# The indexer's scores by pairs of heads: a 128-row matmul each, then a 64-row matmul each, and one PSUM bank moved

## The chip, the cores and the metric

The kernel runs on one core of one Trainium2 chip. The metric is the time of one execution on the device, in microseconds (us). A profile of one execution was taken by the hardware profiler; the engines are PE (TensorE, the matrix engine; PEld are its loads of the stationary operand), DVE (VectorE), ACT (ScalarE), POOL (GpSimd) and SP (SyncE, which here only issues transfers).

## The reference, cut to what matters

One layer of a transformer-like block over 2048 tokens: a first norm and a projection into conv, attention, indexer and pool branches, a sparse attention, an output projection, and a mixture of 32 experts. What is changed lies in the indexer, which picks for each query the 256 keys that attention then uses:

```python
def block(args):
    qa, qib, wib, bi = args
    qchunk = (bi * Q_BLOCK + jnp.arange(Q_BLOCK)) // CHUNK
    allowed = key_chunk[None, :] <= qchunk[:, None]
    rel = jax.nn.relu(jnp.einsum('bqhd,bsd->bqhs', qib, ki).astype(jnp.float32))
    score = jnp.einsum('bqhs,bqh->bqs', rel, wib.astype(jnp.float32)) * idx_scale
    score = jnp.where(allowed[None], score, -jnp.inf)
    _, idx = lax.top_k(score, topk)
...
```

There are 8 indexer heads of 64 channels, 16 tiles of 128 queries, and up to 2048 keys for the last tile.

## The kernel before, in words

The program has five stretches: the projections and the convolution (0 to about 407 us of the profile), the scores of the first tile that needs them ("ahead", inside the last part of the projections, until about 456), the attention (456 to 1225), the output projection and the router (to 1490), and the experts (to the end).

The attention goes over 16 tiles `t` of 128 queries in four groups `g` of two heads each. `attention()` weaves the steps of several generators: `logits(t, g)` of the next group (bank `pl`, three matmuls of `mm3`, lines 92 to 94, then line 1009 on DVE), `context(t, g)` of this group (transposes of line 1032 into bank `pt`, products of line 1044 into bank `pc`, and the 32-column products of line 1051), `scores` of the tile four places on, and `threshold` of tiles between. The tile framework then orders the instructions of each engine by a timeline that it models itself, so the order on PE isn't the order in which the code is written; `order` rows below show it.

`scores(t, S)` works on blocks of up to 512 keys. Queries and keys are held as a sum of two rounded parts, high and low. For an even head, `q[:, h, :]` has the high part on partitions 0 to 63 and the low part on 64 to 127; for an odd head the other way round (`sweep3`). `kk[0]` holds the high part of the keys on both halves of the partitions, `kk[1]` the low part on both. So the matmul of line 843 gives high·high + low·high, and that of line 844 adds high·low + low·low in the same bank. Then ACT takes the relu (line 846) and DVE adds it, weighted, to `S` (line 847).

PSUM has eight banks. The attention uses `pl` x3, `pi` x2, `pt` x2 and `pc` x1:

```python
ps = self.bank("pi", 2)
nc.tensor.matmul(ps[:, :e - s], q[:, h, :], self.kk[0][:, s:e], start=True, stop=False)
nc.tensor.matmul(ps[:, :e - s], q[:, h, :], self.kk[1][:, s:e], start=False, stop=True)
```

`repair()` holds a second copy of the scores' code, which runs only where a query's count of keys came out wrong; it isn't in the trace.

Of the kernel before, what the change touches and what calls it, by code (L numbers as in the profile page):

```python
# [42 lines left out]
def norm_inv(p):  # L43
    """quantile of the standard normal distribution"""
    return NormalDist().inv_cdf(p)


class K:
# [91 lines left out]
    def modulation(self, q, xp):  # L140
        """shift and scale of channels q*256.. by column of 128, for the first norm"""
        nc = self.nc
        acc = xp.tile([128, 2, 256], F32, name="macc", tag="macc", bufs=2)
        for j in range(4):
            w = xp.tile([128, 2, 2, 256], F32, name="modw", tag="xt", bufs=7)
            for m in range(2):
                o = m * D + q * 256
                self.last = nc.sync.dma_start(w[:, :, m], self.a["mod_w"][0, j * 256:(j + 1) * 256, o:o + 256]
                                  .rearrange("(k p) f -> p k f", p=128))
            for i in range(2):  # L150
                k = 2 * j + i
                if k == 0:
                    nc.vector.tensor_scalar(acc, w[:, i], self.cond[:, 0:1], None, op0=OP.mult)
                else:
                    nc.vector.scalar_tensor_tensor(acc, w[:, i], self.cond[:, k:k + 1], acc, op0=OP.mult, op1=OP.add)
        ps = self.cm()
        for m in range(2):
            for j in range(2):
                o = 2 * m + j
                nc.tensor.matmul(ps[:, o:o + 1], acc[:, m, j * 128:(j + 1) * 128], self.ones,  # L160
                                 start=(o == 0), stop=(o == 3), skip_group_check=True)
        s = slice(2 * q, 2 * q + 2)
        nc.vector.tensor_tensor(self.mod.rearrange("p (m k) -> p m k", m=2)[:, :, s],
                                ps[:, :4].rearrange("p (m k) -> p m k", m=2),
                                self.col("mod_b")[:, 0:16].rearrange("p (m k) -> p m k", m=2)[:, :, s], OP.add)
        nc.vector.scalar_tensor_tensor(self.A1[:, s], self.mod[:, 8 + 2 * q:10 + 2 * q], 1.0, self.col("norm1_g")[:, s],
                                       op0=OP.add, op1=OP.mult)

    def modrows(self, mp):
        """the other parts as rows: first gate, second shift and scale (with the norm's gain), second gate"""  # L170
        nc = self.nc
        for i in range(8):
# [13 lines left out]
            ps = self.bank("pl", 3)  # L186
# [18 lines left out]
    def front(self):  # L205
        """x -> normalised, transposed; w_in; conv and pool branches; keys, indexer and queries."""
# [27 lines left out]
    def load_w(self, cols):  # L234
        """column ranges of w_in side by side, [128, KT, n]"""
# [64 lines left out]
    def sweep1(self, c1, u, side):  # L300
        """conv and pool channels: u = a_val sigmoid(a_gate), and u_pool"""
# [88 lines left out]
    def query_weights(self, pool, st):  # L390
        """w_uq[c, h, :] . w_uk[k, h, :] / 8 with both norms' gains, split"""
# [35 lines left out]
    def sweep2(self, c1, side):  # L427
        """keys and values, the indexer's weights and keys, absorbed queries"""
# [14 lines left out]
        def load(t):  # L443
            """h of a tile of tokens"""
# [25 lines left out]
        def turn(c, m):  # L470
            """half of them with channels on partitions"""
# [60 lines left out]
    def spend(self, side, n, after=None):  # L532
        """steps of the convolution, where the engines are free"""
# [7 lines left out]
    def sweep3(self, c1, side):  # L541
        """the indexer's queries: per head, the split halves on partitions 0-63 and 64-127"""
# [32 lines left out]
    def conv(self, st, u):  # L575
        """causal depthwise convolution, layernorm over the channels, silu: a step per yield"""
# [80 lines left out]
    def poolmix(self, st, c, up):  # L657
        """causal moving averages of 2, 4, 8, 16 less the input, a 64x64 product per group"""
# [40 lines left out]
    def work(self, pool, width, dtype, tag, bufs):  # L699
        """a tile of the attention; for the tile of queries that is ahead of it, in the pool that is there"""  # L700
# [6 lines left out]
    def ahead(self):  # L707
        """selection of the first tile of queries that has more than 256 keys, by steps"""
# [36 lines left out]
    def attention(self):  # L745
        nc, tc = self.nc, self.tc
        with ExitStack() as c1:
# [9 lines left out]
            def scores(i):  # L757
                """of the tile at place i, 8 steps per 512 keys"""
# [7 lines left out]
            def bound(i):  # L766
                """its threshold, ten steps; the tiles without one have a plain mask"""
# [31 lines left out]
            for _ in rows:  # L799
# [4 lines left out]
                                   lambda: self.bank("pi", 2, (128, 2, 256)))  # L804
# [19 lines left out]
    def weave(self, *parts):  # L824
        """steps of several generators evenly mixed; the last step of each is its rest"""
# [7 lines left out]
    def scores(self, t, S):  # L833
# [5 lines left out]
        for h in range(NH):  # L839
            for s in range(0, n, 512):  # L840
                e = min(s + 512, n)
                ps = self.bank("pi", 2)
                nc.tensor.matmul(ps[:, :e - s], q[:, h, :], self.kk[0][:, s:e], start=True, stop=False)  # L843
                nc.tensor.matmul(ps[:, :e - s], q[:, h, :], self.kk[1][:, s:e], start=False, stop=True)  # L844
                r = self.work("ap", 512, F32, "rel", 3)
                nc.scalar.activation(r[:, :e - s], ps[:, :e - s], AF.Relu)  # L846
                nc.vector.scalar_tensor_tensor(S[:, s:e], r[:, :e - s], self.wi[:, t, h:h + 1],  # L847
                                               S[:, s:e] if h else self.tie[:, s:e], op0=OP.mult, op1=OP.add)
                yield
# [6 lines left out]
    def plain(self, t):  # L856
        """all the allowed keys, where they are no more than 256"""
# [5 lines left out]
    def threshold(self, t, S):  # L863
        """256 best: counts at moving thresholds until one has 248 to 263 scores above it, then the eight
        next below it or the eight least above it; queries for which that fails are marked"""
# [57 lines left out]
        # from the upper end down (sign 1), or from the lower end up (sign -1) where that is near enough  # L923
# [6 lines left out]
        # which of the eight: 256 - count down, count - 255 up  # L930
# [22 lines left out]
    def repair(self):  # L953
        """tiles with a query whose count is not 256: the selection in order of score and index, and again
        the attention"""
        nc, ap, tc = self.nc, self.ap, self.tc
        ps = self.bank("pl", 3)
# [30 lines left out]
    def logits(self, t, g):  # L988
        """masked logits of two heads, less their maximum, exponentials and their sums"""
# [12 lines left out]
        for h in (2 * g, 2 * g + 1):  # L1002
            L = P[h % 2]
            mx = st[:, 4 * h:4 * h + nb]
            for i, s in enumerate(range(0, n, 512)):
                e = min(s + 512, n)
                ps = self.bank("pl", 3)
# [10 lines left out]
    def context(self, t, g):  # L1018
        """the weighted keys and values of two heads, their outputs"""
# [7 lines left out]
        for k2 in range(0, t + 1, 2):  # L1027
            ks = range(k2, min(k2 + 2, t + 1))
            pt = self.bank("pi" if self.kvs and k2 % 4 else "pt", 2, (128, 2, 2, 128))
# [34 lines left out]
    def output(self):  # L1064
        """mix @ w_out, residual, second norm, router and the experts' lists of tokens"""
# [101 lines left out]
    def mixed(self, c, mix, os_, y, bank):  # L1167
        """conv, attention and pool outputs of 256 tokens, channels on partitions, split"""
# [17 lines left out]
    def blank_lists(self, st):  # L1186
        """the experts' lists full of entries for the spare rows, which are zero"""
# [50 lines left out]
    def first_max(self, st, src, n, N):  # L1238
        """one-hot of the first maximum over the last axis of src [128, N, n], and the maximum"""
# [13 lines left out]
    def route(self, c, lg, st):  # L1253
        """experts and gates of a group of tiles of tokens; their entries go to the experts' lists"""
# [67 lines left out]
    def order(self, st):  # L1322
        """experts by falling number of tokens; the one that is always the first to be computed comes last"""
# [9 lines left out]
        # key: count and, of equal counts, the first expert; by rows over the experts, and as a column  # L1333
# [30 lines left out]
    def parts(self, n):  # L1364
        """n tokens cut into blocks of up to 128, and units of 32 or 64 that share the columns of TensorE with
        other columns of the weights"""
# [10 lines left out]
    def moe_tiles(self):  # L1377
        """the second gate over all the partitions, also by the column groups of the units"""
# [14 lines left out]
    def moe(self):  # L1393
        """the experts in turn, those that TensorE takes longer for mixed with those that the loads take longer
        for; beside the products of the last three the results of all
        the tokens are written, and then again those of the tokens of the three"""
# [72 lines left out]
    def add(self, x):  # L1469
        """the sums into the tokens' rows"""  # L1470
# [3 lines left out]
    def again(self, x):  # L1474
        """the rows of an expert's tokens with the sums so far"""
# [7 lines left out]
    def final_part(self, x, zz, add=False):  # L1483
        """the last norm of an expert's tokens"""
# [22 lines left out]
    def final_rows(self):  # L1507
        """the last norm of all the tokens, by 256"""
# [29 lines left out]
    def gather(self, x, e, N, first):  # L1538
        """the rows of an expert's tokens"""
# [26 lines left out]
    def flip(self, x):  # L1566
        """those rows transposed; those of the blocks also split"""
# [25 lines left out]
    def slot(self, shape):  # L1593
        """the one of eight slots that has been idle for longest; the attention and w_out had them before. Extra
        ones are where the halves of the weights go later"""
# [8 lines left out]
    def done(self, *ws):  # L1604
        """slots whose last use has been written"""
# [4 lines left out]
    def load(self, srcs):  # L1610
        """256 K weights"""
# [22 lines left out]
    def half1(self, m, x):  # L1634
        """half of the inner dimension of the products with w1 and w3 for the blocks, tokens stationary"""
# [25 lines left out]
    def units1(self, x):  # L1661
        """the products with w1 and w3 for the units: a group of TensorE's columns for each part of the hidden
        columns"""
# [21 lines left out]
    def third(self, x, add=True):  # L1685
        """the products with w2, gates, and the sums into the tokens' rows"""
# [59 lines left out]
    def overflow(self):  # L1746
        """experts with more tokens than their part of the plan: 128 at a time"""
# [51 lines left out]
```

## Time and profile before

| what | value |
|---|---|
| time, median of 3 runs | 2300.21 us (2296.73 to 2302.23) |
| span of the profiled execution | 2302.6 us |
| PE busy | 2131.6 us, 93% of the span |
| DVE busy | 1653.4 us, 72% |
| ACT busy | 1233.9 us, 54% |
| POOL busy | 901.8 us, 39% |
| scores on PE: blocks of one head with up to 512 keys | 296 in the attention and 8 before it |

The profiled execution's time is its span; it is 2.4 us (0.1%) above the median of the three runs. The busy time of PE is the union of matmul records, whose ends are modelled: a record of a 512-column matmul is about 0.39 us long, while the next one starts 0.23 us after it. So what a matmul costs is read from start to start.

### The profile page before, as it was taken

How to read it: one execution, taken by the hardware profiler on the slowest of the kernel's cores; microseconds unless marked ns; L12 is line 12 of the kernel's file. 1: busy time of each engine (PE TensorE's matmuls, PEld its weight loads, DVE VectorE, ACT ScalarE, POOL GpSimd, SP SyncE). 2: the span in 40 equal slices, each digit the busy share in tenths (PEclk: the TensorE clock that was granted, in tenths of full speed). 3: DMA queues.
4: the chain of work that ended last, by engine and by line, in shares of the span. 5: the costliest groups of instructions: out<-in, count | busy, mean ns of one | idle time of the engine just before them, and what ended most of it. 6: DMA issues, size and time to landing. Idle time of an engine off the chain costs nothing. (4 is left out here: it accounts for less than half of the span.)

```text
span 2302.6 us, 37318 instructions
## 1 busy us (share of the span) xinstructions
PE 2131.6 (93%) x12943; PEld 1649.6 (72%) x12944; DVE 1653.4 (72%) x3217; ACT 1233.9 (54%) x2078; POOL 901.8 (39%) x1618
## 2 busy tenths in 40 slices
PE   5899999989999999999998999389999999999984
PEld 4777888766777787778897887366776776666763
DVE  5695899578888888887676555585786766766574
ACT  4832331277766667667563222265665665655562
POOL 4532233568745432232000122323565454645344
PEclk9999999999999999999999999689999999999997
DMA  8737869632122232112005644689999999999895
GB/s 282 263 129 229 245 243 325 224 98 65 33 69 83 70 93 83 56 51 62 23 6 206 244 138 138 229 278 309 352 336 293 304 340 346 326 319 323 299 322 169
DMA packets 263902, 460.55 MB, mean 200 GB/s; under 512 B 27985, under 2 KB 123650, under 8 KB 263700
## 3 DMA queue, kind: packets, MB, share of 16 engines
q1 hardware_dynamic: 234324, 363.40, 46.8%
q0 software_dynamic: 26912, 85.19, 12.4%
q10 hardware_dynamic: 2464, 9.44, 1.0%
q8 instruction: 105, 1.72, 0.3%
q14 instruction: 97, 0.79, 0.1%
HBM read 355.48 MB, written 101.43 MB: 198 GB/s over the span
## 5 line engine op out<-in xcount | busy, mean ns | idle before, releaser
L1631 DVE TENSOR_TENSOR wl<-wr,wh 128x1024 fp32r<-128x1024 f32 x314 | 393.0, 1288 | 171.3 <-ACT wh L1630 170.8
L1630 ACT ACTIVATE wh<-wr 128x1024 fp32r<-128x1024 f32 x372 | 373.6, 1053 | 249.2 <-PE acc L94 186.1
L93 PE MATMUL acc<-wl,xh 128*128 128x512 f32 (+3 forms) x544 | 218.7, 403 | 4.9 <-POOL wl L1631 4.7
L92 PE MATMUL acc<-wh,xh 128*128 128x512 f32 (+3 forms) x544 | 216.0, 407 | 5.3 <-ACT wh L1630 3.0
L94 PE MATMUL acc<-wh,xl 128*128 128x512 f32 (+3 forms) x544 | 215.2, 399 | 0.0
L1044 PE MATMUL pc<-pT,kv 128*128 128x256 f32 x840 | 205.1, 385 | 7.2 <-DVE ot L1056 5.6
L1009 DVE CUSTOM_DVE_ANT_0 L<-pl,bias 128x512 f32<-128x512 f32 (+3 forms) x312 | 181.9, 605 | 34.5 <-PE pt L1032 17.2
L846 ACT ACTIVATE rel<-pi 128x512 f32<-128x512 f32 (+3 forms) x296 | 154.5, 548 | 66.0 <-PE pi L844 29.0
L847 DVE SCALAR_TENSOR_TENSOR S<-rel,wi,S 128x512 f32<-128x512 f32 (+3 forms) x259 | 171.3, 679 | 24.1 <-ACT rel L846 23.6
L1044 PEld LDWEIGHTS pc<-pT,kv 128*128 128x128 f32 x840 | 156.3, 192 | 35.8 <-DVE ot L1056 9.4
L1631 POOL TENSOR_TENSOR wl<-wr,wh 128x1024 fp32r<-128x1024 f32 x58 | 145.8, 2562 | 86.0 <-ACT wh L1630 82.8
L1014 ACT ACTIVATE L<-L,ast 128x128 f32<-128x128 f32 (+15 forms) x128 | 154.4, 1207 | 41.6 <-DVE ast L1013 41.4
L598 DVE SCALAR_TENSOR_TENSOR ac<-u,kc,ac 128x512 f32<-128x512 f32 x240 | 174.1, 769 | 0.1
L1032 PE MATMUL pt<-identr,L 128*128 128x128 f32 x968 | 148.3, 275 | 5.2 <-ACT pT L1042 4.5
L1042 ACT ACTIVATE pT<-pt 128x512 f32<-128x512 f32 (+1 forms) x224 | 124.0, 572 | 33.3 <-PE pt L1032 24.3
L843 PE MATMUL pi<-kk,qi 128*128 128x512 f32 (+3 forms) x296 | 127.6, 432 | 14.4 <-ACT rel L846 13.7
L92 PE MATMUL pl<-kvT,qa 128*128 128x512 f32 (+3 forms) x320 | 130.4, 408 | 6.9 <-DVE ast L1009 5.8
L1032 PEld LDWEIGHTS pt<-identr,L 128*128 128x128 f32 x968 | 115.0, 140 | 29.3 <-ACT pT L1042 8.6
L1681 POOL DMA_INDIRECT x_d<-yo,ent x32 | 95.3, 2977 | 89.2 <-DVE yo L1724 66.3
L92 PEld LDWEIGHTS acc<-wh,xh 128*128 128x128 f32 (+3 forms) x544 | 97.5, 182 | 42.6 <-ACT wh L1630 8.7
L93 PEld LDWEIGHTS acc<-wl,xh 128*128 128x128 f32 (+3 forms) x544 | 99.3, 183 | 36.3 <-POOL wl L1631 5.6
L94 PEld LDWEIGHTS acc<-wh,xl 128*128 128x128 f32 (+3 forms) x544 | 99.1, 183 | 27.5
(531 smaller groups left out, 5328.5 us busy)
## 6 DMA issues: line engine op xcount, KB each, us to landing
wr<-in_exp_w_dram SPq DMA_DIRECT2D x256, 512.0 KB
wr<-in_exp_w_dram SPq DMA_DIRECT2D x64, 1024.0 KB
h<-h_d SPq DMA_DIRECT2D x64, 512.0 KB
h_d<-h POOLq DMA_DIRECT2D x32, 512.0 KB
qa_d<-qa POOLq DMA_DIRECT2D x32, 512.0 KB
qa<-qa_d SPq DMA_DIRECT2D x16, 1024.0 KB
modr<-in_mod_w_dram SPq DMA_DIRECT2D x64, 256.0 KB
xt<-in_x_dram SPq DMA_DIRECT2D x16, 512.0 KB
```

Of the source, the lines that this page charges most:

```text
L92: mm(out, lh, rh, start=start, stop=False)
L93: mm(out, lh, rl, start=False, stop=False)
L94: mm(out, ll, rh, start=False, stop=stop)
L598: nc.vector.scalar_tensor_tensor(acc[j], src, kc[:, j, i:i + 1], acc[j], op0=OP.mult, op1=OP.add)
L846: nc.scalar.activation(r[:, :e - s], ps[:, :e - s], AF.Relu)
L847: nc.vector.scalar_tensor_tensor(S[:, s:e], r[:, :e - s], self.wi[:, t, h:h + 1], S[:, s:e] if h else self.tie[:, s:e], op0=OP.mult, op1=O ...
L1009: nc.vector.tensor_tensor_reduce(L[:, s:e], ps[:, :e - s], bias[:, s:e], 1.0, -3e38, OP.add, OP.max, mx[:, i:i + 1])
L1014: nc.scalar.activation(L[:, :n], L[:, :n], AF.Exp, bias=neg, accum_out=st[:, 40 + h:41 + h])
L1032: nc.tensor.transpose(pt[:, kt - k2, j], P[j][:, kt * 128:(kt + 1) * 128], self.ident)
L1044: nc.tensor.matmul(pc, self.kv[:, kt, :], pT[:, kt - k2], start=(kt == 0), stop=(kt == t))
L1630: nc.scalar.activation(H[:, s], W[:, s], AF.Copy)
L1631: (nc.gpsimd if pool else nc.vector).tensor_tensor(L[:, s], W[:, s], H[:, s].bitcast(F32), OP.subtract)
```

## The change

Two heads are now taken together, with two banks `pi`. First come the two matmuls over all 128 rows, as before, then for each head a matmul over the 64 rows on which that head has its high part: rows 0 to 63 for the even head, 64 to 127 for the odd one. The 64-row matmul gives high·low; the product low·low is no longer computed. The number of matmuls and their columns stay as they were. `pi` has three banks in place of two, and `pl` two in place of three, everywhere that these are used. The other lines of the diff only take comments away.

```diff
-        for h in range(NH):
+        mm = nc.tensor.matmul
+        for h in range(0, NH, 2):
             for s in range(0, n, 512):
                 e = min(s + 512, n)
-                ps = self.bank("pi", 2)
-                nc.tensor.matmul(ps[:, :e - s], q[:, h, :], self.kk[0][:, s:e], start=True, stop=False)
-                nc.tensor.matmul(ps[:, :e - s], q[:, h, :], self.kk[1][:, s:e], start=False, stop=True)
-                r = self.work("ap", 512, F32, "rel", 3)
-                nc.scalar.activation(r[:, :e - s], ps[:, :e - s], AF.Relu)
-                nc.vector.scalar_tensor_tensor(S[:, s:e], r[:, :e - s], self.wi[:, t, h:h + 1],
-                                               S[:, s:e] if h else self.tie[:, s:e], op0=OP.mult, op1=OP.add)
-                yield
+                ps = [self.bank("pi", 3)[:, :e - s] for _ in range(2)]
+                for i in range(2):
+                    mm(ps[i], q[:, h + i, :], self.kk[0][:, s:e], start=True, stop=False)
+                for i in range(2):
+                    r = slice(64 * i, 64 * i + 64)
+                    mm(ps[i], q[r, h + i, :], self.kk[1][r, s:e], start=False, stop=True)
+                for i in range(2):
+                    r = self.work("ap", 512, F32, "rel", 3)
+                    nc.scalar.activation(r[:, :e - s], ps[i], AF.Relu)
+                    nc.vector.scalar_tensor_tensor(S[:, s:e], r[:, :e - s], self.wi[:, t, h + i:h + i + 1],
+                                                   S[:, s:e] if h + i else self.tie[:, s:e], op0=OP.mult, op1=OP.add)
+                    yield
...
-                ps = self.bank("pl", 3)
+                ps = self.bank("pl", 2)
...
-            pt = self.bank("pi" if self.kvs and k2 % 4 else "pt", 2, (128, 2, 2, 128))
+            pt = self.bank("pi" if self.kvs and k2 % 4 else "pt", 3 if self.kvs and k2 % 4 else 2, (128, 2, 2, 128))
```

The same moves of a bank (`pl` 2, `pi` 3) are made in `modrows`, `repair` and the call of `mixed`. In the changed file, line 845 is the 128-row matmul, line 848 the 64-row one, 1037 the transposes (1032 before), 1049 the products with `kv` (1044 before) and 1056 the 32-column products (1051 before).

The first place is the start of the attention on PE, its first four matmuls of scores; `pi_...` is the bank of a head's block, `kk0` and `kk1` are the high and low keys, `pl_...` the bank of the logits. Before:

```order
L843 MATMUL pi_4208<-kk0_1770,qi_4206 128x512
L844 MATMUL pi_4208<-kk1_1771,qi_4206 128x512
L843 MATMUL pi_4214<-kk0_1770,qi_4206 128x512
L844 MATMUL pi_4214<-kk1_1771,qi_4206 128x512
L92 MATMUL pl_4268<-kvT0_1772,qa_4263 128x128
```

And in the change, the same place:

```order
L845 MATMUL pi_4208<-kk0_1770,qi_4206 128x512
L845 MATMUL pi_4209<-kk0_1770,qi_4206 128x512
L848 MATMUL pi_4208<-kk1_1771,qi_4206 128x512
L848 MATMUL pi_4209<-kk1_1771,qi_4206 128x512
L845 MATMUL pi_4220<-kk0_1770,qi_4206 128x512
L848 MATMUL pi_4220<-kk1_1771,qi_4206 128x512
L92 MATMUL pl_4268<-kvT0_1772,qa_4263 128x128
```

Here the first pair stands as the code has it, with its two 64-row matmuls one behind the other; the next head's two already stand alone.

The second place is on PE in the middle of the attention of the change, between the logits (`pl`), the 32-column products (line 1056) and the transposes (`pt`):

```order
L94 MATMUL pl_7034<-kvT0_1772,qa_6540 128x384
L1056 MATMUL pc_4204<-wv_3275,cT_6785 32x64 x8
L845 MATMUL pi_6942<-kk0_1770,qi_6660 128x512
L848 MATMUL pi_6942<-kk1_1771,qi_6660 128x512
L845 MATMUL pi_6983<-kk0_1770,qi_6660 128x512
L848 MATMUL pi_6983<-kk1_1771,qi_6660 128x512
L1037 MATMUL pt_6950<-identr_130,L_6820 128x128
```

The 128-row and the 64-row matmul of each head stand together, and a 128-row one lies between the two 64-row ones of a pair. Of the 304 matmuls of line 848 in the part that runs, 5 stand directly in front of another of them; 179 stand in front of a matmul of lines 845, 92 or 93, 101 in front of one of lines 1037, 1049 or 618 (transposes and the products with `kv`), 16 in front of line 1056 and 3 in front of line 187 (one column).

## Rows read from the trace of the kernel before

**Rows 1.** Busy time by stage: us, busy by engine (instructions), clock, DMA share, GB/s.
```profile
456.00:1046.00 590.00, 554.33 (x3559) 442.98 (x3559) 489.43 (x1283) 413.83 (x819) 277.18 (x942) 0.99 0.24 71
1046.00:1225.00 179.00, 177.66 (x1322) 157.03 (x1320) 122.30 (x311) 109.85 (x162) 16.09 (x75) 1.00 0.10 32
```

**Rows 2.** Waits of PE from 456 to 1046: us in total, times, longest.
```profile
PE pi L843 <- ACT rel L846: 13.7, 18, 3.1
PE pl L92 <- DVE ast L1009: 5.8, 11, 1.3
PE pc L1044 <- DVE ot L1056: 5.6, 7, 1.9
PE pt L1032 <- ACT pT L1042: 4.5, 6, 1.2
...
PE pl L187 <- DVE ast L1009: 0.2, 1, 0.2
```

**Rows 3.** The scores' matmuls by shape, 456 to 1046: xcount, busy us, mean ns.
```profile
L844 PE MATMUL pi<-kk,qi 128*128 128x512 f32 x224 | 88.8, 396 | 0.0
...
L844 PE MATMUL pi<-kk,qi 128*128 128x384 f32 x24 | 8.1, 338 | 0.0
...
L844 PE MATMUL pi<-kk,qi 128*128 128x256 f32 x24 | 6.8, 282 | 0.0
L844 PE MATMUL pi<-kk,qi 128*128 128x128 f32 x24 | 6.6, 275 | 0.0
```

**Rows 4.** Timeline of PE: start us, us, what (rows*columns), matrix, xcount.
```profile
567.58 0.60 PE L1032 MATMUL pt<-identr,L 128*128 128x128 f32 x4
568.11 0.41 PE L1051 MATMUL pc<-wv,cT 128*32 128x64 f32 x10
568.45 0.50 PE L843 MATMUL pi<-kk,qi 128*128 128x512 f32 x1
568.78 0.40 PE L844 MATMUL pi<-kk,qi 128*128 128x512 f32 x1
569.11 0.31 PE L1051 MATMUL pc<-wv,cT 128*32 128x64 f32 x6
569.35 0.50 PE L92 MATMUL pl<-kvT,qa 128*128 128x512 f32 x1
569.69 0.40 PE L93 MATMUL pl<-kvT,qa 128*128 128x512 f32 x1
569.93 0.39 PE L94 MATMUL pl<-kvT,qa 128*128 128x512 f32 x1
```

**Rows 5.** Timeline of PE's loads in the same stretch.
```profile
569.11 0.15 PEld L1051 LDWEIGHTS pc<-wv,cT 128*32 128x32 f32 x6 [0.36 <-issue]
569.35 0.19 PEld L92 LDWEIGHTS pl<-kvT,qa 128*128 128x128 f32 x1
569.46 0.19 PEld L93 LDWEIGHTS pl<-kvT,qa 128*128 128x128 f32 x1
```

**Rows 6.** Timeline of PE: two transposes over 31 rows, then 128-row matmuls.
```profile
98.12 0.31 PE L583 MATMUL cm<-identr,kr 31*128 31x31 f32 x2
98.35 0.50 PE L92 MATMUL sm<-h,wh 128*128 128x512 f32 x1
98.69 0.40 PE L93 MATMUL sm<-h,wh 128*128 128x512 f32 x1
98.92 0.39 PE L94 MATMUL sm<-h,wl 128*128 128x512 f32 x1
```

**Rows 7.** Timeline of PE: 64-row products of line 419, then transposes.
```profile
235.41 2.79 PE L419 MATMUL sm<-ukT,uqT 64*128 64x128 f32 x32 [1.74 <-DVE ukT L410]
238.13 0.66 PE L483 MATMUL sm<-identr,z 128*128 128x128 f32 x4
```

**Rows 8.** Busy time of line 419 on PE: stretch, us, busy (matmuls), clock, DMA.
```profile
235.93:236.50 0.57, 0.57 (x12) 1.00 1.19 299
...
235.40:236.00 0.60, 0.59 (x6) 1.00 1.15 289
```

**Rows 9.** DVE's costliest lines that read the bank of the logits, 456 to 1046.
```profile
L1009 DVE CUSTOM_DVE_ANT_0 L<-pl,bias 128x512 f32<-128x512 f32 (+3 forms) x226 | 127.8, 585 | 7.7 <-PE pl L94 6.7 <-DMA y_d<-ac 0.6 <-PE pt L1032 0.2
...
L1009 DVE DVE_READ_ACCUMULATOR2_ANT ast<- 128x1 f32 x234 | 19.0, 81 | 0.0
```

More of the change, by code (lines that the diff above doesn't have):

```diff
@@ L803, in attention @@
                                    ap.tile([128, 4, 256], F32, name="cj", tag="cj", bufs=3),
-                                   lambda: self.bank("pi", 2, (128, 2, 256)))
+                                   lambda: self.bank("pi", 3, (128, 2, 256)))
             self.W = [self.w_cut(self.w_load(k, ap), self.ats, *tag) for k, tag in enumerate((("S", 3), ("R", 1)))]
@@ L956, in repair @@
         nc, ap, tc = self.nc, self.ap, self.tc
-        ps = self.bank("pl", 3)
+        ps = self.bank("pl", 2)
         nc.tensor.matmul(ps[0:1, 0:NT], self.ones, self.bad, start=True, stop=True)
@@ L1006, in logits @@
                 e = min(s + 512, n)
-                ps = self.bank("pl", 3)
+                ps = self.bank("pl", 2)
                 self.mm3(ps[:, :e - s], q[:, h, 0], q[:, h, 1], self.kvT[0][:, s:e], self.kvT[1][:, s:e], True, True)
```

## The prediction

> **What bounds the kernel now.** I read busy time by stage first. The scores run between 456 and 1046 us; in these 590 us PE is busy for 554, DVE for 489, ACT for 414 [rows 1]. Then comes what PE waited for: its waits, ten entries, sum to 34.7 us, which is nearly the whole of its 35.7 idle, and the longest entry is the scores' own bank, 13.7 us until ACT's relu had emptied it [rows 2]. So the stage is PE's, with some 6% of slack, and what PE spends longer is paid nearly in full. The weights of the experts come into buffers that the attention uses until its end, so a longer attention moves all that follows; I expect no change in the length of later stages.
>
> What one matmul costs is read from start to start. Within the logits, line 93 starts at 569.69 and line 94 at 569.93: 0.24 us for 512 columns, with the load of the stationary operand hidden beside the matmul before [rows 4]. In the scores there are 304 blocks, 296 in this stage (224 with 512 columns, three times 24 with 384, 256 and 128) [rows 3] and 8 with 384 columns before it.
>
> **The change part by part.** Matmuls, columns, relus and sums stay as many as they were. What could be saved is the overlap of the two 64-row matmuls of a pair. That such matmuls do overlap the trace shows in line 419, the only 64-row products: with one half of the rows at work 6 start in 0.60 us, with both halves 12 in 0.57 [rows 8]. If all 152 pairs did so, one half matmul of each would vanish: 112 pairs at 0.23 us, 16 at 0.175, 12 at 0.12 and 12 at 0.06, 30.7 us in all (0.23 scaled by columns). But a 128-row matmul needs both halves, and in the order of the change one lies between the two of a pair in all but 5 pairs. The saving is then 5 x 0.2 = 1 us.
>
> What it adds is a change of how the array is divided, from 128 rows to 64 and back, at each of the 299 places where 64-row matmuls begin and end. The trace of before has such changes at the 32-column products. Line 844 starts at 568.78, line 1051 behind it at 569.11: 0.33 in place of 0.23 to 0.24, so PE pauses 0.10 before the first 32-column matmul [rows 4]. On the way back line 92 starts at 569.35 and line 93 at 569.69, 0.34 in place of 0.24: the load of line 92 begins only at 569.35 and that of line 93 at 569.46, so 0.10 of load lies open which is hidden elsewhere [rows 4, 5]. The 31-row transposes do the same: the second starts near 98.20 and has at most 0.06 of work, line 92 starts at 98.35, and line 93 0.34 behind it, against 0.23 from there to line 94 [rows 6]. And at the end of the 64-row products: the last record ends at 238.20 and is 0.27 long, so it starts at 237.93; the transposes start 0.20 later, where 128 columns cost 0.11 [rows 7, 8]. That is the same pause of 0.09, though a wait on PE's own semaphore stands there too. That four transposes then take 0.66, against 0.60 in line 1032, prices the open load before them at 0.06 [rows 4, 7].
>
> One page speaks against the change outright: the Trainium skill, "TensorEngine Tiling (Array Packing)", section "Tiling Modes", says that a change of tiling mode, other than a change of tile, drains the engine. The pauses at 32 columns and 31 rows agree with it; it names no price, and the entry into 64 rows behind a 128-row matmul is in no row here. By the rule there is a pause at every entry and exit, without it none.
>
> I take the entry like that into 32 columns, since the exits of rows and columns agree to about 0.01 us: pause 0.10 and open load 0.10. The sum:
>
> - 299 entries x 0.20 = 59.8 us (no load can hide, since the 64-row operand can't be loaded while the array still works on 128 rows).
> - Exits: 179 in front of lines 845, 92, 93 x 0.20 = 35.8; 101 in front of transposes and the products with kv x (0.10 + 0.06) = 16.2; 19 in front of line 1056 or 187, which pause already, 0.
> - Overlap in 5 pairs: -1.
>
> Together +111 us. Bounds of one switch: below, nothing, if a change of rows costs nothing in one direction; above, the 0.20 that the rows show.
>
> What hides of it: a pause that falls where PE waits anyway is free. The waits are 35 us [rows 2], and as PE gets 18% more to do while ACT and DVE keep their work, waits shrink. Between 0 and 35 I take half, -18. The third bank `pi` aims at the 13.7 us of these and is in that bound.
>
> The second bank `pl` that is left: DVE takes 0.585 + 0.081 = 0.67 us per block on average [rows 9], PE's three matmuls about 0.70 for 512 columns; the wait for it is 5.8 us now [rows 2]. Nothing at the low end; at the high end the read of the accumulator, 0.08, lies open in each of 226 blocks, 18 us. In the new order matmuls of other lines, now slower, lie between, so I take +3. From 1046 to 1225, where logits run without scores, PE is busy for 177.7 of 179 [rows 1] with DVE at 122, so there is little to win and a few us to lose, within the same bound.
>
> Sum: 111 - 18 + 3 = +96. The profiled execution (2302.6) gives 2398.6; it stands 2.4 above the median of 2300.2, to which I set the forecast: **2396 us**.
>
> **The rivals.**
>
> *Faster: the halves overlap without a pause.* All 152 pairs give 30.7 us: 2270. Line 419 speaks for it, with a half that starts while the other works [rows 8]; it needs the two 64-row matmuls of a pair behind one another, and the order has that in 5. It decides if the array lets a 64-row matmul run beside a 128-row one on the other half. Of packing into rows, the Trainium skill, "TensorE: Matmul & The Clock Gate", "Part 3: Packing small matmuls", reports 3.07 times the speed with four row tiles. That holds for tiles one behind the other; by it all pairs overlapping would give this rival's time, and rows 8 agree with a factor near 2 for two halves.
>
> *Nothing: rows switch without a pause.* The 64-row matmul then costs what the 128-row one does, since the columns are the same, and only the banks and 1 us of overlap count: -14 from `pi` to +18 from `pl`, so 2286 to 2318, about 2299. For it: the entry into 64 rows isn't shown. Against it: the exit is, twice [rows 6, 7].
>
> *Half: only the exit, or only the entry, pauses.* 52 or 60 us, less the half of the waits: 2300 + 56 - 18 + 3 = 2341. For it, again, that only exits are seen with rows; against it, that with columns both directions pause [rows 4].
>
> *Slower through the banks alone* would be the upper end of the second rival, 2318.
>
> **How the numbers follow.** Pauses at both ends 0.80, one end 0.08, none 0.07, overlap 0.05. The first alone reaches from 2300 + 111 - 35 = 2376, a little lower if waits of the third bank vanish with it (2362), to 2300 + 111 + 18 = 2429. To leave out no more than 2 in 10 the range goes down to the half case: 2341 to 2429. The time of this kernel can be told from no change at about 0.2% (4.6 us); of the case without pauses I give 0.02 to faster, 0.03 to the same and 0.02 to slower. So faster 0.07, same 0.03, slower 0.90.
>
> **What would show it.** In the timeline of PE line 848 starts, with its load, about 0.33 after a line 845 that had its load hidden and 0.43 after one that came out of a switch itself (0.23 if nothing pauses); the matmul behind line 848 starts 0.43 after it, and its own successor 0.34 later. The stage of the scores grows from 590 to about 685 us, while the stages behind it keep their lengths; the waits of line 845 for ACT get fewer. The five pairs that stand together start their halves within about 0.01 us. The prediction is wrong if line 848 follows at 0.23 (no pause), or if PE's waits for `pl` come to more than 18 us; and if the clock, 0.99 of full in this stage [rows 1], falls in the pauses, the time is above the range.

## The result, and the profile after

The changed kernel takes 2364.5 us (median of 4 runs, 2358.2 to 2370.8) against 2300.4 us of before measured beside it: 1.0277 times, 95% interval 1.0254 to 1.0300, so 64 us slower. The forecast was 2396 in a range of 2341 to 2429, slower with a chance of 0.90. The direction and the mechanism came out; the size was 32 us too large. The times in this text leave out the slow executions, of which there were two, both of the logits' bank alone (2430 and 2651 us, at a granted clock of 0.84 and 0.75 where the others have 0.97). The two executions that the profiles show, of 2302.6 and 2359.5 us, lie 57 us apart: the one of before was a little longer than its median, the one of the change a little shorter.

The timeline of PE in the middle of the scores of the changed kernel (start us, us, what; line 848 is the 64-row matmul):

```profile
700.06 0.50 PE L845 MATMUL pi<-kk,qi 128*128 128x512 f32 x1
700.49 0.50 PE L848 MATMUL pi<-kk,qi 64*128 64x512 f32 x1
700.91 0.50 PE L92 MATMUL pl<-kvT,qa 128*128 128x512 f32 x1
701.25 0.39 PE L93 MATMUL pl<-kvT,qa 128*128 128x512 f32 x1
701.47 0.39 PE L94 MATMUL pl<-kvT,qa 128*128 128x512 f32 x1
...
704.13 0.39 PE L845 MATMUL pi<-kk,qi 128*128 128x512 f32 x1
704.45 0.50 PE L848 MATMUL pi<-kk,qi 64*128 64x512 f32 x1
704.88 2.43 PE L1049 MATMUL pc<-pT,kv 128*128 128x256 f32 x10
```

Read from start to start. Behind a line 845 that comes out of the logits, and so had its load hidden, line 848 starts after 0.32 (704.13 to 704.45), not after 0.23: the pause. Behind one that comes out of a switch itself it starts after 0.43 (700.06 to 700.49). The matmul behind line 848 starts 0.42 to 0.43 later, and line 93 starts 0.34 behind line 92, against 0.22 from there to line 94. PE's loads in the same stretch say why:

```profile
700.48 0.18 PEld L848 LDWEIGHTS pi<-kk,qi 64*128 64x128 f32 x1 [0.24 <-issue]
700.91 0.19 PEld L92 LDWEIGHTS pl<-kvT,qa 128*128 128x128 f32 x1 [0.24 <-issue]
701.02 0.19 PEld L93 LDWEIGHTS pl<-kvT,qa 128*128 128x128 f32 x1
701.25 0.19 PEld L94 LDWEIGHTS pl<-kvT,qa 128*128 128x128 f32 x1
```

The load for the first matmul in the other division (line 848, then line 92) begins only when that matmul's turn has come, after 0.24 in which no load ran; the load of line 93, in the same division, begins 0.11 later, beside the matmul of line 92. This is the pattern that [rows 4 to 6] showed for 32 columns and 31 rows.

The first pair of the attention is one of the five whose halves stand together:

```profile
459.61 0.49 PE L848 MATMUL pi<-kk,qi 64*128 64x512 f32 x2
460.03 0.50 PE L845 MATMUL pi<-kk,qi 128*128 128x512 f32 x1
```

Two matmuls take 0.49, no more than one record, and the next starts 0.42 behind the first: the halves do overlap. In the trace they start 0.003 us apart.

Busy time by stage of the changed kernel, with the scores in the first row and the rest of the attention in the second (us, busy of PE, PEld, DVE, ACT and POOL, clock, DMA):

```profile
459.00:1012.00 553.00, 551.45 (x3022) 371.10 (x3022) 446.66 (x1131) 376.52 (x746) 282.49 (x941) 1.00 0.22 64
1012.00:1284.00 272.00, 264.61 (x1868) 226.60 (x1872) 169.98 (x461) 152.59 (x234) 22.56 (x75) 0.99 0.14 44
```

The same of before, cut where its scores end:

```profile
456.00:1044.00 588.00, 552.33 (x3549) 441.22 (x3550) 487.43 (x1277) 411.83 (x816) 277.18 (x942) 0.99 0.24 71
1044.00:1226.00 182.00, 180.57 (x1353) 159.58 (x1351) 124.38 (x318) 111.85 (x165) 16.09 (x75) 1.00 0.10 31
```

Before, the attention lasted 770 us with PE busy for 732.9; now it lasts 825 with PE busy for 816.1. So PE's busy time grew by 83 us and its idle time fell from 37 to 9. The granted clock, 0.99 to 1.00 in all four stretches, is not the cause. One sign did not come out: the stretch of the scores was to grow from 590 to about 685 us, and it shrank to 553, because the scores now end at 1012 us in place of 1044. What grew is the rest of the attention, from 182 to 272 us. The kernel with the banks alone, below, shows the same shift. What follows the attention keeps its length: 2302.6 - 1226 = 1077 us before, 2359.5 - 1284 = 1076 after. PE's listed waits up to 1107 us are down to six entries of 7.0 us in all, the first of which is

```profile
PE pl L92 <- DVE ast L1014: 3.8, 2, 3.0
```

and the 13.7 us for the scores' bank [rows 2] are 0.6. Instead DVE now waits for PE's logits: 105 us over the attention, where it was 16. Only a part of that comes from the switches: it is 66.5 us with the banks moved alone and 43.7 us with the rows changed alone.

```profile
DVE L L1014 <- PE pl L94: 105.4, 97, 3.0
```

### The profile page after: what moved, and what is told of

Read it like the earlier page. It is cut to its first block, busy times and chain, and to the rows that moved or that the text cites. A ratio compares the mean times of both kernels' runs of the same rounds, so it can differ in the third digit from the quotient of the medians.

```text
span 2359.5 us, 37345 instructions
## 1 busy us (share of the span) xinstructions
PE 2217.5 (94%) x12943; PEld 1647.0 (70%) x12944; DVE 1662.6 (70%) x3217; ACT 1240.4 (53%) x2078; POOL 914.5 (39%) x1618
## 5 line engine op out<-in xcount | busy, mean ns | idle before, releaser
L1014 DVE CUSTOM_DVE_ANT_0 L<-pl,bias 128x512 f32<-128x512 f32 (+3 forms) x312 | 187.0, 608 | 113.1 <-PE pl L94 103.4
L1037 PE MATMUL pt<-identr,L 128*128 128x128 f32 x968 | 154.9, 279 | 2.4 <-ACT L L1019 1.8
L92 PE MATMUL pl<-kvT,qa 128*128 128x512 f32 (+3 forms) x320 | 139.8, 437 | 3.9 <-DVE ast L1014 3.8
L848 PE MATMUL pi<-kk,qi 64*128 64x512 f32 (+3 forms) x296 | 136.6, 468 | 0.0
```

The source lines that it names most:

```text
L92: mm(out, lh, rh, start=start, stop=False)
L1014: nc.vector.tensor_tensor_reduce(L[:, s:e], ps[:, :e - s], bias[:, s:e], 1.0, -3e38, OP.add, OP.max, mx[:, i:i + 1])
L1037: nc.tensor.transpose(pt[:, kt - k2, j], P[j][:, kt * 128:(kt + 1) * 128], self.ident)
```

## The experiments

Two theories stood against each other. The first: the switches between 128 and 64 rows cost PE a pause and an open load each, and the stage is PE's. The rival: what costs is the bank taken from the logits, or the pairs and the order that follows from them. Every kernel was timed in five rounds against the kernel before on the same chip, whose medians there were 2301.3 to 2302.3 us.

**The banks alone.** The kernel before, with

```diff
-                ps = self.bank("pi", 2)
+                ps = self.bank("pi", 3)
...
-                ps = self.bank("pl", 3)
+                ps = self.bank("pl", 2)
```

> The kernel before with nothing but the PSUM banks moved (logits 2, scores 3). If the slow-down comes from the switches between 128 and 64 rows, this kernel stays within 0.4% of before: 2292 to 2309 us, with PE's pauses as before. If the lost bank of the logits is what costs, it is slow like the change: above 2330 us, with waits of line 92 for line 1009 of more than 18 us.

Measured: 2323.5 us, 1.0109 (1.0091 to 1.0126). Both miss. The banks don't explain the change, but they cost 22 us where I had counted 3. The wait of line 92 for line 1009 is only 7.6 us, the wait for the scores' bank is longer with three banks than with two (20.9 against 13.7 [rows 2]), and DVE waits for the logits for 66.5 us in place of 16.2. The scores end at 937 us in place of 1044:

```profile
453.00:937.00 484.00, 440.42 (x2793) 351.05 (x2794) 418.33 (x1065) 347.89 (x713) 299.63 (x941) 0.98 0.23 68
937.00:1246.00 309.00, 300.50 (x2097) 254.60 (x2098) 194.60 (x528) 172.17 (x267) 17.68 (x75) 0.99 0.15 46
```

DVE is at 86% in the first stretch and at 63% in the second (before: 83% and 68%), PE sits idle for 44 us in the first and 8 in the second (before: 36 and 1). Its busy time for the same matmuls is 8 us longer, 740.9 against 732.9.

**The logits' bank alone.** The kernel before with `self.bank("pl", 2)` and the scores' two banks as they were; one PSUM bank stays unused.

> The kernel before with two banks for the logits and still two for the scores: seven banks in use. Moving both banks cost 22 us. If the lost bank of the logits costs that, this kernel is at 2310 to 2330 us. If the third bank of the scores does (it lets them run ahead, so that they end 107 us earlier and DVE is denser in front), this kernel is at 2296 to 2306 us.

Measured: 2309.5 us, 1.0033 (1.0021 to 1.0044), between the two expectations and 0.5 us below the first: 8 of the 22 us come with the loss of the logits' bank. The other 14 come when the scores get that bank, which was meant to help. The third bank of the scores by itself, with three for the logits, would need nine banks and was not run.

**The pairs with 128 rows.** The change, with

```diff
-                    mm(ps[i], q[r, h + i, :], self.kk[1][r, s:e], start=False, stop=True)
+                    mm(ps[i], q[:, h + i, :], self.kk[1][:, s:e], start=False, stop=True)
```

> The change with its second matmul over all 128 rows again (low times low comes back); pairs, banks and nearly the order stay. If the switches cost, the whole +62 us goes: 2290 to 2312 us, and the second matmul starts 0.23 us behind the first. If pairs, banks or the order cost, it stays above 2330 us.

Measured: 2317.7 us, 1.0065 (1.0052 to 1.0078). Most of the slow-down goes, but 15 us stay, 6 us more than I had allowed for. The banks alone cost 22, so the pairs add nothing to them, and the 15 us are most likely the banks'. The pairs over 128 rows with the banks of before were not run, so this is not shown by itself.

**The rows alone.** The kernel before, with

```diff
-                nc.tensor.matmul(ps[:, :e - s], q[:, h, :], self.kk[1][:, s:e], start=False, stop=True)
+                r = slice(64 * (h % 2), 64 * (h % 2) + 64)
+                nc.tensor.matmul(ps[:, :e - s], q[r, h, :], self.kk[1][r, s:e], start=False, stop=True)
```

> The kernel before with one edit: the second matmul over the 64 rows that hold the head's high part (low times low is left out); one head at a time, banks and the order on PE are those of before. If the switches cost, it is as slow as the change or a little slower, since no two 64-row matmuls stand together: 2352 to 2385 us. If the pairs or the banks cost, it is at 2300 us.

Measured: 2355.0 us, 1.0231 (1.0218 to 1.0244), as the first theory has it. This is the cleanest pair of kernels: the order on PE through the attention is the same, matmul by matmul (4896 of them), and only the number of rows differs. In the profiled execution the scores start at 462 us, 6 later than before. By stage from there:

```profile
462.00:1097.00 635.00, 634.88 (x3548) 439.82 (x3548) 494.47 (x1277) 428.83 (x815) 257.25 (x941) 1.00 0.22 66
1097.00:1279.00 182.00, 180.81 (x1350) 159.60 (x1349) 124.46 (x317) 112.04 (x165) 16.05 (x75) 1.00 0.10 31
```

PE's busy time grows by 815.7 - 732.9 = 83 us, its idle time falls from 37 to 1.3, and the attention is 47 us longer. The other 6 us lie before it.

**Half as many of them.** The kernel before, 64 rows for heads 0 to 3 only:

```diff
-                r = slice(64 * (h % 2), 64 * (h % 2) + 64)
+                r = slice(64 * (h % 2), 64 * (h % 2) + 64) if h < 4 else slice(0, 128)
```

> The kernel before with the 64-row second matmul for heads 0 to 3 only (low times low is left out there); the order on PE is that of before. All eight heads cost 54 us. If the pauses first fill PE's waits (37 us in before, under 2 us with all heads) and only what is above them is paid, half the heads cost clearly less than half: 8 to 20 us. If a fixed share of each pause is hidden, they cost half: 23 to 31 us.

Measured: 2320.1 us, 1.0090 (1.0072 to 1.0107): 21 us by the ratio, 39% of the 53 for all heads, at the upper edge of the first expectation; the interval (17 to 25 us) reaches into the second, so the time alone does not settle it. The stages do, in one execution of each kernel:

```profile
459.00:1058.00 599.00, 589.42 (x3547) 440.74 (x3547) 489.26 (x1276) 418.65 (x816) 270.81 (x942) 1.00 0.24 69
1058.00:1240.00 182.00, 180.66 (x1341) 159.71 (x1343) 124.92 (x318) 112.48 (x165) 16.01 (x75) 1.00 0.10 31
```

PE's busy time is up by 770.1 - 732.9 = 37 us and its idle time is down by 37 - 11 = 26, so the attention is 11 us longer, against 47 with all heads. The first half of the switches takes up 26 us of idle time, the second half only 9 more: the waits fill up, and what comes after is paid.

**The banks as before in the change.** `pl` 3 and `pi` 2 again, pairs and 64 rows as changed.

> The change with the banks of before (logits 3, scores 2). If banks and switches add up, it loses the 15 to 22 us of the banks and is near the kernel of before with 64 rows alone: 2338 to 2356 us. If the pauses of the switches have already eaten the slack that the banks cost, nothing changes: 2358 to 2370 us.

Measured: 2349.6 us, 1.0211 (1.0192 to 1.0231), inside the first expectation. The banks are worth 15 us in the change too, and without them it is nearly as slow as the rows alone (2355.0), so the pairs cost nothing here either.

**The halves together.** The change, with the second matmuls held behind the first ones of both heads:

```diff
                 for i in range(2):
-                    mm(ps[i], q[:, h + i, :], self.kk[0][:, s:e], start=True, stop=False)
-                for i in range(2):
-                    r = slice(64 * i, 64 * i + 64)
-                    mm(ps[i], q[r, h + i, :], self.kk[1][r, s:e], start=False, stop=True)
+                    whole = mm(ps[i], q[:, h + i, :], self.kk[0][:, s:e], start=True, stop=False)
+                with self.tc.issue_after(whole.ins):
+                    for i in range(2):
+                        r = slice(64 * i, 64 * i + 64)
+                        mm(ps[i], q[r, h + i, :], self.kk[1][r, s:e], start=False, stop=True)
```

> The change with one constraint on PE's order: both 64-row matmuls of a pair come behind both 128-row ones, so all 152 pairs stand together. Switches halve, and the second half starts within 0.01 us of the first. From the rows: 152 entries at 0.20 and exits at about 0.19 are 59 us, 30 us of matmuls vanish, +29 us, most of which the waits of before (36 us) could hide unless the pair's wait for two banks brings new ones: 2295 to 2325 us. If the halves do not overlap on the chip, +59 us: 2330 us or more. If a pair that stands together is worth what the change was made for, it is under 2285 us.

Measured: 2322.3 us, 1.0082 (1.0068 to 1.0095), inside the first expectation, near its upper end. The order that the code suggests takes away 42 of the 64 us, but not all. In its timeline the pair is one record long, as in the first pair above:

```profile
708.47 0.47 PE L845 MATMUL pi<-kk,qi 128*128 128x512 f32 x1
708.87 0.50 PE L849 MATMUL pi<-kk,qi 64*128 64x512 f32 x2
709.30 0.50 PE L845 MATMUL pi<-kk,qi 128*128 128x512 f32 x1
```

**Together, on the same half.** Both heads on rows 0 to 63, so that the halves can't overlap; the odd head's second product is then low·low.

```diff
-                        r = slice(64 * i, 64 * i + 64)
+                        r = slice(0, 64)
```

> The halves together, but both heads of a pair use rows 0 to 63 (the odd head then gets low times low in place of high times low). Order and switches are those of the halves together (2322 us); only the overlap of two halves of the array goes. If overlap gives 30 us of PE's work back, most of it on the path since the stage is PE's, this kernel is at 2337 to 2355 us, and the second half starts 0.2 us behind the first. If overlap was worth little, it stays under 2330 us.

Measured: 2337.1 us, 1.0164 (1.0150 to 1.0179), 15 us above the halves together and at the lower end of the first expectation. The order on PE in the attention is that of the halves together, matmul by matmul.

```profile
705.71 0.73 PE L849 MATMUL pi<-kk,qi 64*128 64x512 f32 x2
706.37 0.66 PE L1038 MATMUL pt<-identr,L 128*128 128x128 f32 x4
```

From the start of the pair to what follows it takes 0.66 us (705.71 to 706.37), where the halves together took 0.43 (708.87 to 709.30). The difference, 0.23, is one 512-column matmul. The second matmul itself starts 0.34 behind the first, not the 0.2 that was expected: the first one's load lies open for 0.10, which the halves together pay too. PE is busy for 784.5 us of the attention in place of 749.7. So the overlap is real: it gives back 35 us of PE's busy time, 15 of them in time.

**Together, over 128 rows.** The second matmuls again behind both first ones, with neither switches nor overlap. All 152 pairs stand together here too, but the rest of PE's order is not the same as with the halves together.

> The pairs with both second matmuls behind both first ones, all of them over 128 rows: the same order as in the kernel with the halves together, with neither switches nor overlap. If a pair that stands together costs +28 us of switches less 30 us of overlap, that is about nothing, this kernel is within 10 us of the one with the halves together (2322): 2312 to 2332 us. If the switches weigh more than the overlap gives back, it is at 2300 to 2312 us.

Measured: 2314.1 us, 1.0047 (1.0030 to 1.0065), inside the first expectation. Against the halves together (1.0082) it is 8 us faster, with intervals that just miss each other. PE is busy for 736.8 us of the attention against 749.7, so with both halves side by side the switches still cost more than the overlap gives back. The attention itself differs by only 3 us in the two profiles (783 against 786), and since the order differs too, the 8 us are not all shown to be switches.

**Together, with the banks as before** (`pl` 3, `pi` 2).

> The halves together, with the banks of before (logits 3, scores 2, both taken by one pair). If the banks were what kept the halves together above before, it is at 2295 to 2312 us, the best form of the change. If a pair that needs both banks of the scores at once waits for the relus of the pair before, with line 845 waiting for line 852 for 30 us or more, it is above 2320 us.

Measured: 2324.9 us, 1.0097 (1.0077 to 1.0117). The second expectation by its time, but not for its reason: line 845 waits for the relu for 7.1 us only, and the largest wait of PE is another one, 10.5 us in front of the 32-column products. No form of the change that was tried beats the kernel before.

## Why the prediction was right, and where its sizes were off

The switches are the cause. The rows alone, in an unchanged order, give 53 of the 64 us, and taking the rows back in the change takes 47 away. The step that decided it, that an entry into 64 rows costs what an entry into 32 columns does, was an inference from columns, since no row of before had it; the timeline confirms it to 0.01 us (pause 0.09 to 0.10, open load 0.10 to 0.11). The rivals "nothing" and "half" fall with the same rows: line 848 does not follow at 0.23, and both ends pause. The rival "overlap" had its mechanism right and its place wrong: halves overlap where they stand together, which is in 5 pairs.

The range held the time partly by luck. By its own sum the case that came true reached down to 2376 us, or to 2362 if the waits of the third bank vanished with the rest. The measured 2364 lies at the bottom of that; the range reached further only because it was drawn down to the half case. Two sizes of the sum were off.

- *What the waits hide.* I took half of 35 us, and 35 as the most that could hide. Where the order is the same, the two traces can be compared matmul by matmul. Take for each matmul, by its neighbours and columns, the median from its start to the next start, in the rows alone and in before: the difference, summed over the attention, is about 102 us of switches. This is an estimate from these two traces. My prices give 108 for the same order (59 for the entries, 34 and 15 for the exits), so the price of the switches was right. But the attention grew by only 47 us, so some 55 were hidden. Of these, 35 are idle time of PE that vanished, 37 to 1.3. The other 20 are waits that never showed as idle time: the record of a 512-column matmul is 0.39 us long and the next can start at 0.23, so a wait of up to 0.16 behind it counts as busy. That is also why PE's busy time grew by 83 us and not by 102. The step that was mis-sized is the upper bound of 35, read from idle time. (A slip beside it: 111 us on 554 are 20% more for PE, not 18%.)
- *The banks.* I took +3 with a range of -14 to +18. They cost 22 us without switches and 15 with them, and not by the way that I had named: PE's waits for `pl` are 7.6 us with the banks alone and 3.8 in the change. This error ran against the other one, so the forecast was closer than its terms: without the banks' term it would have been 2393, and the rows alone measured 2355.

The prices of the exits can be read one by one. In before, and at the same place with the rows alone (line 845 is the 64-row matmul there, line 1033 the transpose):

```profile
822.88 0.39 PE L844 MATMUL pi<-kk,qi 128*128 128x512 f32 x1
823.11 0.27 PE L1032 MATMUL pt<-identr,L 128*128 128x128 f32 x1
823.14 0.47 PE L93 MATMUL pl<-kvT,qa 128*128 128x512 f32 x1
```

```profile
853.84 0.50 PE L845 MATMUL pi<-kk,qi 64*128 64x512 f32 x1
854.27 0.33 PE L1033 MATMUL pt<-identr,L 128*128 128x128 f32 x1
854.36 0.48 PE L93 MATMUL pl<-kvT,qa 128*128 128x512 f32 x1
```

The second matmul takes 0.43 in place of 0.23 up to the transpose, and the transpose 0.09 in place of 0.03: the 0.06 that I had charged. Behind an exit in front of the products with kv the next start comes after 0.32 in place of 0.22 (medians of the change), more than that 0.06.

Why a third bank makes the scores slower is not settled. It lets them end 107 us earlier, with DVE denser in front and PE waiting more there. Among the kernels without switches an earlier end of the scores mostly goes with a later end of the attention (1044 and 1226 us before, 1005 and 1232 with two logits' banks, 964 and 1241 with the pairs over 128 rows, 937 and 1246 with both banks moved). The pairs held together over 128 rows, with 1013 and 1239, do not fit, and no run changed the one alone.

## What to carry to other kernels

A matmul over fewer rows costs its columns all the same, and where it stands between matmuls over all rows it costs two switches more, here 0.2 us each, so that each is nearly as much as a 512-column matmul (0.23). Packing two halves pays only if they stand together and the stretch in the other division is long enough to pay for its entry and exit; a pair of 512-column halves was not here, and a longer stretch was not tried. Look at the order that the scheduler makes, not at the code: it took the pairs apart in 147 of 152 cases. And in a stage that one engine fills to 94%, added work on that engine is hidden by its waits only until these are gone. There can be more of them than the idle time shows, where the records of an engine overlap: here about 55 us were hidden and 37 were idle.

## What was not expected of the hardware

The price of a switch was the same for rows as for 32-column groups within 0.01 us, in the two places where both can be read: the pause at the entry (0.09 to 0.10) and the open load behind the exit (0.10 to 0.11). Two 64-row matmuls on different halves, each into a bank of its own, took the time of one: 0.43 us up to what follows, against 0.66 on the same half. The Trainium skill, "TensorEngine Tiling (Array Packing)", section "Tiling Modes", states that a change of tiling mode drains the engine and that different tiles can load and multiply in parallel. The trace agrees with both, and it gives the price of the first: a pause of 0.10 us, and a load of 0.10 us that lies open behind it.
